# Squaring a second copy of the input: the head of a fused attention-and-experts block on one core

## Chip, cores and metric

The kernel runs on one core of a Trainium2 chip. The metric is the device time of one execution in microseconds (us), as the median of several executions. The profile shows one execution, taken by the hardware profiler.

## What is computed

One layer over 512 tokens of width 2048, all in float32. The part that matters here is its very beginning: the input is normalised and multiplied by a wide matrix, whose columns are then split into many projections.

```python
def rmsnorm(t, g):
    tf = t.astype(jnp.float32)
    y = tf * lax.rsqrt(jnp.mean(tf * tf, axis=-1, keepdims=True) + EPS)
    return (y * g.astype(jnp.float32)).astype(t.dtype)

def reference(x, positions, norm_mix_g, w_in, ...):
    ...
        h = rmsnorm(x, norm_mix_g[l])
        proj = jnp.einsum('bsd,de->bse', h, w_in[l])
        c_q, c_kv, k_rope, dq, dk, dv, iq, ik, iw, gates = jnp.split(proj, splits, axis=-1)
        o_a = mla_branch(c_q, c_kv, k_rope, ...)          # latent attention
        o_b = dsa_branch(dq, dk, dv, iq, ik, iw, ...)     # index scores, top-k, sparse attention
        gate = jax.nn.sigmoid(gates) ...
        merged = gate[:, :, 0, :] * (o_a @ w_branch_a[l]) + gate[:, :, 1, :] * (o_b @ w_branch_b[l])
        x = x + merged @ w_out[l]
        x = x + peer_ffn(rmsnorm(x, norm_ffn_g[l]), ...)  # 16384 experts, 128 picked per token
    return rmsnorm(x, norm_final_g)
```

## The kernel before

The tokens are worked in two halves of 256 (`HB`). `projections(i, ...)` does one half; `i = 0` is the first thing that the kernel does, and the change touches only that half, apart from a step that is written so that the second half keeps its place.

**Two-part products.** A float32 matrix product is made of three matmuls on rounded operands: a value is a high part (`hi`, a rounded copy, type fp32r) plus a low part (`lo`, what the rounding lost). `mm3` (L139 to L142) issues the three. `wload` (L106) loads a block of weights into `raw` (a ring of 4 buffers), lets ScalarE (ACT) make `hi` (ring of 4, L114) and VectorE (DVE) make `lo` (ring of 3, L115). `xraw` (L118) loads into the same `raw` ring without the split. Both are marked as high priority.

**Who sets the order.** The program is written as a stream of operations. A scheduler orders each engine's queue: among the operations that it takes to be ready it picks the one that comes first in the program, with the high-priority ones ahead. On the chip each engine then works its queue strictly in order. SyncE (SP) issues nearly all loads, in its own order.

**The first stage, for the first half.** Sixteen slices `k` of the transposed input (128 features x 256 tokens) come in four loads `in_xt` of 512 KB, and the weights of the first projection, `in_wdv`, in six loads. For each slice:

- ACT makes `hT` (L471), the high part of the slice times the gain `gmix`
- ACT makes `h1` (L473), an unsplit copy of the second 128 tokens of the same product, for the index queries further on
- DVE makes `lT` (L475), the low part
- ACT squares the slice (L478), and DVE adds the square to `sq` (L480)
- TensorE (PE) multiplies `hT` and `lT` with the weights into `pd` (L140 to L142 with 272 columns, 96 matmuls in all, two blocks of 128 tokens)

The gain is in `hT`, but 1/rms is not. It is found while PE goes on: one product with `ones` (`prr`, L505) sums `sq` over the partitions, `rstd_of` (L144 to L155) makes 1/rms of it on DVE and ACT, and the result lies in `rrow` (L507). Each later projection of this half is multiplied by `rrow` as it is read (`scaled`, L424).

After that stage the program has `angles(0)` and `angles(1)` (sines and cosines for the rotations; `angles(2)` stands inside the first stage, behind its first chunk, L481 to L487), then the projections. A projection chunk `proj_chunk` (L403) is 48 matmuls of 256 columns into `pm`, which has two buffers (tag `mm`; one of them is shared with `pd`). The first chunk is `W_KRIK` (result `xk`, followed by rotations L321 to L331), then the two gate chunks of feature block 0 (`gate`, L446), then eight index-query chunks with unsplit weights and `h1` (L546).

## Time and profile before

| | us |
|---|---|
| median of 3 runs | 3571.36 |
| the three runs | 3570.12, 3571.36, 3579.55 |
| the profiled execution, its time | 3575.54 |
| the profiled execution, its span | 3573.8 |

The span is from the first to the last instruction; 1.7 us lie around it. In the tables PE is TensorE's matmuls and PEld its weight loads, ACT ScalarE, DVE VectorE, SP SyncE (SPq its queue of DMA issues), PEclk the granted clock of TensorE as a share of full speed. L140 is line 140 of the kernel. A row of the timeline has start, duration, engine, line, operation, output and inputs, shape, count; in square brackets the idle time of the engine before it and what ended it. Durations are from start to end of an instruction, and neighbours on an engine overlap, so that the pitch (start to start) is shorter.

### The profile page before, as it was taken

The page shows a single profiled execution, that of the slowest core. Times are in us where ns is not written, and L with a number is a line of the kernel's source. Part 1 is how long each engine was busy: PE and PEld are TensorE (multiplying, and loading weights), DVE is VectorE, ACT ScalarE, POOL GpSimd, SP SyncE. Part 2 cuts the span into 40 slices and gives each one's busy share as a digit, 9 for nine tenths or more (in the row PEclk, how much of TensorE's full clock was granted, in tenths as well). Part 3 has the DMA queues.
Part 4 walks back from the last instruction along what each step waited for, and adds up shares of the span by engine and source line. Part 5 has one row for each costly group of instructions (what it writes and reads, how often), then busy time and mean ns, then how long its engine had stood idle before and what let it go on. Part 6 is the DMA issues. An engine that isn't in the chain of part 4 may idle for free.

```text
span 3573.8 us, 55133 instructions
## 1 busy us (share of the span) xinstructions
PE 3389.8 (95%) x20917; PEld 3041.6 (85%) x20917; DVE 2804.6 (78%) x4658; ACT 1428.7 (40%) x2195; POOL 581.8 (16%) x388
## 2 busy tenths in 40 slices
PE   8999899999889789899999999998999999999996
PEld 7999798778788679779999999998878778788885
DVE  6864565589997569878998887876878789788797
ACT  5454644443121453343354544543323233233232
POOL 0000000000222022210001111110322224223222
PEclk9999999999999989999999999999999999999998
DMA  6576267544999458976788888888989899999997
GB/s 221 187 227 207 73 208 243 168 148 174 346 369 393 171 193 339 355 293 223 250 308 313 330 328 325 325 320 332 367 321 346 328 365 349 354 357 352 355 357 284
DMA packets 282681, 1027.77 MB, mean 288 GB/s; under 512 B 29488, under 2 KB 98736, under 8 KB 228656
## 3 DMA queue, kind: packets, MB, share of 16 engines
q1 hardware_dynamic: 193712, 567.04, 45.1%
q0 software_dynamic: 55296, 402.68, 29.3%
q10 hardware_dynamic: 33408, 54.54, 4.1%
q8 instruction: 164, 2.69, 0.3%
q14 instruction: 101, 0.83, 0.1%
HBM read 962.80 MB, written 58.72 MB: 286 GB/s over the span
## 4 chain that ended last, share of the span: by engine, by line
PE 74%; DVE 11%; DMA 10%; ACT 2%; issue 2%; SPq 0%; ACTq 0%; DVEq 0%
PE pv L141 8%; PE pv L142 8%; PE pv L140 8%; PE pu L142 5%; PE pu L140 5%; PE pu L141 5%; PE pm L140 5%; PE pm L142 5%; PE pm L141 5%; PE pm L409 3%; DVE r L269 3%; DVE lo L115 3%; DMA gt<-g_d 3%; PE pg L939 2%; DMA raw<-in_win 2%
## 5 line engine op out<-in xcount | busy, mean ns | idle before, releaser
L114 ACT CAST hi<-raw 128x1024 fp32r<-128x1024 f32 (+2 forms) x836 | 873.4, 1049 | 1363.9 <-PE pv L142 298.5
L115 DVE TENSOR_TENSOR lo<-raw,hi 128x1024 fp32r<-128x1024 f32 (+2 forms) x836 | 1015.4, 1218 | 459.2 <-issue 128.2
L267 POOL DMA_INDIRECT r<-in_u,idx x256 | 367.7, 1436 | 2480.0 <-DVE dots L269 1397.5
L141 PE MATMUL pv<-lo,ch 128*128 128x512 f32 x1536 | 599.6, 392 | 18.9 <-DVE lo L115 18.8
L142 PE MATMUL pv<-hi,cl 128*128 128x512 f32 x1536 | 592.3, 391 | 0.0
L269 DVE CUSTOM_DVE_ANT_0 r<-r,h2g 128x2048 f32<-128x2048 f32 x256 | 582.3, 2284 | 10.0 <-DMA r<-in_u,idx 8.1
L140 PE MATMUL pu<-h2h,hi 128*128 128x256 f32 x1888 | 542.5, 287 | 10.8 <-ACT hi L114 8.3
L140 PE MATMUL pv<-hi,ch 128*128 128x512 f32 x1536 | 543.5, 391 | 2.3 <-ACT hi L114 1.6
L142 PE MATMUL pu<-h2h,lo 128*128 128x256 f32 x1888 | 533.9, 283 | 0.8 <-DVE lo L115 0.8
L141 PE MATMUL pu<-h2l,hi 128*128 128x256 f32 x1888 | 534.2, 283 | 0.0
L140 PE MATMUL pm<-hT,hi 128*128 128x256 f32 x1240 | 365.7, 295 | 18.0 <-ACT xi L421 7.7
L142 PE MATMUL pm<-hT,lo 128*128 128x256 f32 x1240 | 358.4, 289 | 14.2 <-DVE lo L115 14.2
L140 PEld LDWEIGHTS pu<-h2h,hi 128*128 128x128 f32 x1888 | 358.5, 190 | 12.0 <-ACT hi L114 8.5
L141 PEld LDWEIGHTS pv<-lo,ch 128*128 128x128 f32 x1536 | 290.2, 189 | 86.3 <-DVE lo L115 26.0
L142 PEld LDWEIGHTS pu<-h2h,lo 128*128 128x128 f32 x1888 | 358.3, 190 | 1.2 <-DVE lo L115 1.1
L141 PEld LDWEIGHTS pu<-h2l,hi 128*128 128x128 f32 x1888 | 358.5, 190 | 0.6
L141 PE MATMUL pm<-lT,hi 128*128 128x256 f32 x1240 | 355.0, 286 | 0.0
L140 PEld LDWEIGHTS pv<-hi,ch 128*128 128x128 f32 x1536 | 288.9, 188 | 64.2 <-ACT hi L114 2.9
L142 PEld LDWEIGHTS pv<-hi,cl 128*128 128x128 f32 x1536 | 290.1, 189 | 59.9
L282 DVE SCALAR_TENSOR_TENSOR hacc<-r,dots,hacc 128x2048 f32<-128x2048 f32 x128 | 300.4, 2347 | 9.7 <-DMA r<-in_v,idx 9.6
L280 POOL DMA_INDIRECT r<-in_v,idx x128 | 214.0, 1672 | 486.3 <-DVE hacc L282 393.0
L140 PEld LDWEIGHTS pm<-hT,hi 128*128 128x128 f32 x1240 | 239.2, 193 | 22.8 <-ACT xi L421 8.5
(396 smaller groups left out, 5278.6 us busy)
## 6 DMA issues: line engine op xcount, KB each, us to landing
raw<-in_ut SPq DMA_DIRECT2D x256, 512.0 KB
raw<-in_vd SPq DMA_DIRECT2D x256, 512.0 KB
raw<-in_win SPq DMA_DIRECT2D x228, 512.0 KB
raw<-in_wbr SPq DMA_DIRECT2D x64, 512.0 KB
raw<-in_wo SPq DMA_DIRECT2D x64, 512.0 KB
g_d<-gs ACTq DMA_DIRECT2D x24, 1024.0 KB
gt<-g_d SPq DMA_DIRECT2D x8, 3072.0 KB
raw<-in_wq SPq DMA_DIRECT2D x32, 512.0 KB
```

The costliest lines, as they stand in the source:

```text
L114: nc.scalar.copy(hi, raw)
L115: latest[0] = nc.vector.tensor_sub(lo, raw, hi.bitcast(F32))
L140: nc.tensor.matmul(ps, wh, xh, start=first, stop=False)
L141: nc.tensor.matmul(ps, wh, xl, start=False, stop=False)
L142: nc.tensor.matmul(ps, wl, xh, start=False, stop=last)
L267: nc.gpsimd.indirect_dma_start(out=r, out_offset=None, in_=a["u"], in_offset=bass.IndirectOffsetOnAxis(ap=idx[b][:, j:j + 1], axis=0))
L269: nc.vector.tensor_tensor_reduce(out=r, in0=r, in1=h2g[b], scale=1.0, scalar=0.0, op0=ALU.mult, op1=ALU.add, accum_out=dots[b][:, j:j + 1])
L280: nc.gpsimd.indirect_dma_start(out=r, out_offset=None, in_=a["v"], in_offset=bass.IndirectOffsetOnAxis(ap=idx[0][:, j:j + 1], axis=0))
L282: nc.vector.scalar_tensor_tensor(acc, r, dots[0][:, j:j + 1], acc, ALU.mult, ALU.add)
L409: nc.tensor.matmul(pm, w[:, j * P:(j + 1) * P], hF[:, j, :], start=False, stop=j == 7)
L939: end[0] = nc.tensor.matmul(pg[:, j], o2[:, j, :], og[:, j, :], start=True, stop=True)
```

## The change

It has five parts, all for the first half.

1. The squares (L478) and their additions (L480) leave the loop over the slices. Behind the first products the four blocks `in_xt` are loaded a second time, squared and added up.
2. The first two projection chunks (`W_KRIK` and the first gate chunk) are put ahead of that in the program, and so ahead of the product with `ones`.
3. The copy of `pd` into `dvw` (L518) is put ahead of these two chunks, as the second needs the buffer that `pd` holds.
4. The unsplit copy `h1` is no longer made by ACT from the input, but by DVE as `hT + lT`, behind the two gate chunks.
5. `angles(2)` with its loads (`fr`, `ident`, positions) stands behind the chunk of slices 12 to 14, no longer behind that of slices 0 to 2.

```diff
-                def gate(f, br):
+                def gate(f, br, pm=None):
...
-                    scaled(sg, proj_chunk(W_G + 2 * f + br), AF.Sigmoid)
+                    scaled(sg, pm or proj_chunk(W_G + 2 * f + br), AF.Sigmoid)
...
                             nc.scalar.activation(hT[:, k, :], x_, AF.Copy, scale=gmix[:, k:k + 1])
-                            if i == 0:
-                                nc.scalar.activation(h1[:, k, :], x_[:, P:], AF.Copy, scale=gmix[:, k:k + 1])
-                            if k < ks:
-                                nc.vector.scalar_tensor_tensor(lT[:, k, :], x_, gmix[:, k:k + 1], hT[:, k, :].bitcast(F32),
-                                                               ALU.mult, ALU.subtract)
-                            s2 = sq if k == 0 else dq[:, 4 + k % 4, :]
-                            nc.scalar.activation(s2, x_, AF.Square)
-                            if k:
-                                nc.vector.tensor_add(sq, sq, s2)
-                        if k0 == K_A:
+                            nc.vector.scalar_tensor_tensor(lT[:, k, :], x_, gmix[:, k:k + 1], hT[:, k, :].bitcast(F32),
+                                                           ALU.mult, ALU.subtract)
+                        if k0 == (0 if i else 12):
...
                     if i == 0:
+                        for j, tb in enumerate(blocks):
+                            nc.scalar.copy(dvw[:, tb, :], pd[j])
+                        first = [proj_chunk(m) for m in (W_KRIK, W_G)]
+                        for k in range(KT):
+                            if k % 4 == 0:
+                                xt = xraw(a["xt"][0, k // 4])
+                            s2 = sq if k == 0 else dq[:, 4 + k % 4, :]
+                            nc.scalar.activation(s2, xt[:, (k % 4) * HB:(k % 4 + 1) * HB], AF.Square)
+                            if k:
+                                nc.vector.tensor_add(sq, sq, s2)
                         pr = ps.tile([P, S], F32, name="prr", tag="tr")[:, :HB]
                         nc.tensor.matmul(pr, ones, sq, start=True, stop=True)
...
-                        nc.scalar.copy(dvw[:, tb, :], pd[j])
...
-                scaled(xk, proj_chunk(W_KRIK))
+                scaled(xk, proj_chunk(W_KRIK) if i else first[0])
...
                 for f in range(GF):
-                    gate(f, 0)
+                    gate(f, 0, None if i else first[1])
                     gate(f, 1)
+                if i == 0:
+                    for k in range(KT):
+                        nc.vector.tensor_add(h1[:, k, :], hT[:, k, P:].bitcast(F32), lT[:, k, P:].bitcast(F32))
```

## Rows read from the trace of the kernel before

**Rows 1.** The page: the span, and busy time of the engines with their share of the span.

```profile
span 3573.8 us, 55133 instructions
PE 3389.8 (95%) x20917; PEld 3041.6 (85%) x20917; DVE 2804.6 (78%) x4658; ACT 1428.7 (40%) x2195; POOL 581.8 (16%) x388
```

**Rows 2.** Busy time by stretch of the span: the stretch, its length, then busy us and count of PE, PEld, DVE, ACT and POOL, the granted clock, the share of the DMA engines and GB/s.

```profile
0.00:20.00 20.00, 9.91 (x54) 9.46 (x54) 14.28 (x36) 16.04 (x40) 0.20 (x4) 1.00 0.74 250
20.00:40.00 20.00, 17.54 (x130) 16.22 (x131) 17.24 (x29) 17.57 (x32) 0.00 (x0) 1.00 0.68 224
...
60.00:80.00 20.00, 19.96 (x148) 17.56 (x146) 9.85 (x36) 5.07 (x16) 0.00 (x0) 1.00 0.75 241
```

**Rows 3.** Timeline of PE: the first matmul, the first after the change of pitch, the waits of the first stage, the last product of `pd` and the first of `pm`, the product for 1/rms, the last of the second chunk, and the first rotation.

```profile
9.09 0.59 PE L140 MATMUL pd<-hi,hT 128*128 128x272 f32 x1 [9.09 <-ACT hT L471]
...
14.69 0.40 PE L140 MATMUL pd<-hi,hT 128*128 128x272 f32 x1
...
18.65 0.29 PE L142 MATMUL pd<-hi,lT 128*128 128x272 f32 x1
18.77 0.29 PE L140 MATMUL pd<-hi,hT 128*128 128x272 f32 x1
18.90 0.29 PE L141 MATMUL pd<-lo,hT 128*128 128x272 f32 x1
...
27.81 0.52 PE L140 MATMUL pd<-hi,hT 128*128 128x272 f32 x2 [1.15 <-ACT hi L114]
28.18 0.70 PE L505 MATMUL prr<-dq,ones 128*128 128x256 f32 x2
...
29.22 0.28 PE L140 MATMUL pm<-hT,hi 128*128 128x256 f32 x1
...
30.23 0.29 PE L140 MATMUL pm<-hT,hi 128*128 128x256 f32 x1
...
41.16 0.28 PE L142 MATMUL pm<-hT,lo 128*128 128x256 f32 x1
42.63 0.70 PE L321 MATMUL prot<-xk,cm 128*128 128x256 f32 x2 [1.19 <-DVE xk L424]
```

**Rows 4.** Groups of instructions by line and form, from 0 to 43 us: count, then busy us and mean ns of one, then idle time before them and what ended it.

```profile
L471 ACT ACTIVATE hT<-raw,gmix 128x256 fp32r<-128x256 f32 x16 | 7.9, 494 | 0.0
L475 DVE SCALAR_TENSOR_TENSOR lT<-raw,gmix,hT 128x256 fp32r<-128x256 f32 x16 | 7.5, 481 | 0.2 <-ACT hT L471 0.2
L480 DVE TENSOR_TENSOR dq<-dq 128x256 f32<-128x256 f32 x15 | 6.3, 422 | 0.5
L473 ACT ACTIVATE h<-raw,gmix 128x128 f32<-128x128 f32 x16 | 6.2, 386 | 0.0
L478 ACT ACTIVATE dq<-raw 128x256 f32<-128x256 f32 x16 | 6.0, 403 | 1.0 <-DMA raw<-in_xt 1.0
```

**Rows 5.** Timeline of ACT: the first split of weights, the second input block's first square and the first `hT`, and one later chunk of slices.

```profile
4.24 0.87 ACT L114 CAST hi<-raw 128x816 fp32r<-128x816 f32 x1 [2.22 <-DMA raw<-in_wdv]
...
8.22 0.42 ACT L478 ACTIVATE dq<-raw 128x256 f32<-128x256 f32 x1 [0.63 <-DMA raw<-in_xt]
8.54 0.49 ACT L471 ACTIVATE hT<-raw,gmix 128x256 fp32r<-128x256 f32 x1
...
24.05 0.49 ACT L471 ACTIVATE hT<-raw,gmix 128x256 fp32r<-128x256 f32 x1
24.45 0.39 ACT L473 ACTIVATE h<-raw,gmix 128x128 f32<-128x128 f32 x1
24.74 0.40 ACT L478 ACTIVATE dq<-raw 128x256 f32<-128x256 f32 x1
25.05 0.49 ACT L471 ACTIVATE hT<-raw,gmix 128x256 fp32r<-128x256 f32 x1
```

**Rows 6.** Timeline of DVE from the product for 1/rms to the first projection that it scales, with the first and the last of the five passes of `lo` between.

```profile
29.88 0.42 DVE L148 TENSOR_SCALAR rv<-prr 128x256 f32<-128x256 f32 x1
30.21 1.22 DVE L115 TENSOR_TENSOR lo<-raw,hi 128x1024 fp32r<-128x1024 f32 x1
31.34 0.35 DVE L434 TENSOR_SCALAR dq<-dq,fr 128x256 f32<-128x256 f32 x1
...
33.79 1.75 DVE L150 RECIPROCAL ry<-ry 128x256 f32<-128x256 f32 x1 [0.30 <-ACT ry L149]
...
39.08 1.22 DVE L115 TENSOR_TENSOR lo<-raw,hi 128x1024 fp32r<-128x1024 f32 x1
...
42.16 0.42 DVE L424 TENSOR_TENSOR xk<-pm,rrow 128x256 f32<-128x256 f32 x1
```

**Rows 7.** Timeline of SP: issues of the first input and weight blocks.

```profile
0.75 0.39 SPq L111 DMA_DIRECT2D raw<-in_wdv  x1
...
2.12 0.43 SPq L121 DMA_DIRECT2D raw<-in_xt  x1
2.60 0.53 SPq L401 DMA_DIRECT2D gmix<-in_gmix  x1
```

**Rows 8.** DMA from 0 to 120 us: GB/s in 40 slices of 3 us, and the total.

```profile
GB/s 91 384 372 368 154 125 188 223 179 158 274 343 236 240 158 0 44 113 273 287 288 203 225 268 229 204 295 173 264 301 349 261 190 180 156 172 68 220 116 202
DMA packets 9552, 25.73 MB, mean 214 GB/s; under 512 B 1552, under 2 KB 3344, under 8 KB 9542
```

**Rows 9.** A later place where PE waits (timeline of PE), and three stretches there with the columns of rows 2.

```profile
415.67 0.71 PE L640 MATMUL po<-pT,va 128*128 128x128 f32 x4 [0.39 <-ACT pT L638]
419.80 0.47 PE L355 MATMUL psc<-kr,two 128*128 128x128 f32 x1 [3.42 <-DMA two<-qrl]
...
420.00:424.00 4.00, 4.00 (x13) 3.08 (x13) 1.60 (x11) 1.80 (x7) 0.00 (x0) 0.50 0.00 0
...
428.00:432.00 4.00, 4.00 (x23) 4.00 (x24) 1.84 (x12) 3.33 (x12) 0.00 (x0) 0.58 0.00 0
430.00:434.00 4.00, 4.00 (x33) 4.00 (x31) 2.00 (x12) 3.81 (x15) 0.00 (x0) 0.83 0.00 0
```

**Rows 10.** Two neighbouring DVE operations on 128 x 128 elements in the index-query stage.

```profile
54.55 0.28 DVE L339 TENSOR_TENSOR rt<-xi,trig 128x128 f32<-128x128 f32 x1
54.75 0.28 DVE L340 TENSOR_TENSOR rt<-rt,trig 128x128 f32<-128x128 f32 x1
```

## The prediction

> **What bounds the kernel now.** I read the page first: PE is busy 95% of the span [rows 1], so over the whole kernel a change counts only where PE waits or runs slowly. The diff touches only the first 50 us or so, so I read that stretch next, by the table of stretches. From 60 us on PE is busy all the time (19.96 of 20 us), from 0 to 20 it is busy 9.91 and from 20 to 40 it is busy 17.54, with ACT at 16.04 and 17.57 and DVE at 14.28 and 17.24 [rows 2]. So what happens before PE becomes the bound moves the end by the same amount, and nothing later gives it back.
>
> The timeline of PE says how much there is to win [rows 3]. PE's first matmul is at 9.09; the first rotation, which needs `xk` and so 1/rms, is at 42.63, and from there PE is full again. I take 42.63 as the mark: what the change does to it is what it does to the time. Between lie 33.54 us. The work in them, at the fast pitch: 96 matmuls of `pd` at 0.125 (18.65, 18.77, 18.90) are 12.0; 96 of the two chunks at 0.1175 (from 30.23 to 41.16 are 93 steps) are 11.3; the two of `prr` are 0.7. That is 24.0. The first 24 matmuls ran at a pitch of 0.23, from 9.09 to 14.69, 5.6 us where the fast pitch needs 3.0: 2.6 more. So 33.54 - 24.0 - 2.6 = 6.9 us are waits and gaps, 1.2 of them the last wait, for `xk`. **No version of this stage that starts at 9.09 can win more than 6.9 us, 0.19% of the time.** What a measurement of this kernel can tell from no change is about 0.3%, or 10.7 us.
>
> **Part by part.** *ACT in the first stage.* For each slice ACT makes `hT`, `h1` and the square, at pitches of 0.40, 0.29 and 0.31: 24.05 to 25.05, 1.00 us for a slice [rows 5]. The change leaves 0.40. Sixteen slices lose 9.6 us of ACT, and DVE loses 15 additions [rows 4] at a pitch of about 0.34, 5.1 us. For a chunk of three slices ACT then needs about 0.77 + 1.2 = 2.0 us against 18 x 0.125 = 2.25 of PE. So ACT, which most of PE's waits in this stage named, falls behind PE as the bound. The start stays: the first `hT` at 8.54 stands behind a square that waited for the second input block, but the load of `gmix`, which `hT` needs, was issued behind that block [rows 5, 7]; at most 0.3 us are to be had, and I take none. With the slow clock until 14.69 and 72 matmuls left, `pd` ends at 14.69 + 9.0 = 23.7 at the earliest, where the last ended at 29.2. Gain 5.5 at most; I take 4.5 for waits that stay, since loads and the split on DVE have the same rate as PE now. The bounds are 3.5 and 5.5.
>
> *The two chunks* need 11.3 us whether they run before or behind `prr`. They end at 35.0 at the earliest, 37.0 at the latest; I take 36.0.
>
> *The product for 1/rms.* Before, it ran at 28.18, among the last matmuls of `pd`, and everything that follows from it lay under the two chunks [rows 3, 6]. Now it stands behind them in the program. Their matmuls are ready all the time, and an engine's queue takes the earlier in the program first, so I place it behind the second chunk: 36.0 to 36.7. The squares are there by then: `raw` has four buffers, and a weight block leaves its buffer when `lo` is made, which needs one of three `lo` buffers, so the fourth weight block goes when PE is through the first half chunk, 2.8 us behind 24.7, at 27.5. The last input block is issued then. The nearest load with nothing ahead of it took from 0.75 to 4.24, 3.5 us [rows 5, 7]; 31.0, and four squares and an addition are 1.6 more: 32.6. These 2 MB hide under the chunks with 3 us to spare.
>
> *The chain behind it.* From 29.88 to the end of `xk` at 42.58 are 12.7 us, but five passes of `lo` on DVE lie between its links, of about 1.14 pitch each, 5.7 us [rows 6]. In the changed order no weight block waits to be split at that point, as the next blocks with a split are few and early and the index queries have none. So 7.0 is the upper bound. The links alone are `rv` 0.42, the square root 0.42, 1.75 for the reciprocal, four more short operations of 1.3 together, the copy 0.28 and `xk` 0.42, in sum about 4.6, with steps between engines 4.8: the lower bound. I take 6.2, nearer to the upper, as sines and cosines still fill DVE's holes. Now nothing covers it: PE has no other buffer for `pm`, and the third chunk waits for `xk`. So `prr` begins at 36.0, 0.7 + 6.2 + 0.1 later the rotation: 43.0, or **0.4 later than before**. By the bounds it is 35.0 + 5.6 = 40.6 (2.0 earlier) to 37.0 + 7.8 = 44.8 (2.2 later).
>
> *The clock in that wait.* PE stands idle 5 to 7 us. The nearest row is a wait of 3.42 us up to 419.80, behind which the granted clock is 0.50, that is 1.2 GHz, until some 431, then 2.4 GHz [rows 9]. So I expect half speed behind the new wait. What it costs is bounded by two rows: the start, 2.6 us more over 5.6 us of full work [rows 3], and that later place, where some 11.7 us at half clock would cost 5.9 for full work [rows 9]. The third chunk is full work as at the start, so I take 2.5.
>
> The Trainium skill, "TensorE: Matmul & The Clock Gate", section "What's actually happening", says that the throttled state is the default and that activity releases it; so a wait does more harm than its length. The trace agrees at 419.80 (0.50 after 3.42 us of idling). By that rule the sum is 2.9 us later; if the clock stayed at full the rotation's 0.4 would be all.
>
> *`h1` on DVE.* Sixteen additions of 128 x 128 at a pitch of 0.20 [rows 10] are 3.2 us; they must be done when the index queries start, about 8 us behind the rotation. They need only `hT` and `lT`, so DVE's holes during the chunks and the chain can take them. I take zero; uncovered they cost up to 3.2.
>
> *The other edits* move `angles(2)` and the copy of `pd`. The sines are wanted only at the rotation, and the copy (two ACT operations) comes before the second chunk needs its buffer, 6 us later: nothing, and at most the 1.3 us by which a table load for the sine could hold a split.
>
> **Sum.** -4.5 for `pd`, + 11.3 + 0.7 and a chain that is no longer under the chunks: together +0.4 at the rotation; +2.5 for the clock; 0 for `h1`: **+2.9 us**. Against the profiled execution's 3575.5 that is 3578.4, against the median of the runs, which is 4.2 lower, 3574.3. I forecast 3575 us, no change that can be measured. Its own range is -2.0 to +8.1 on these two bases, some 3569 to 3583.
>
> **Rivals.**
>
> *The early result.* 1/rms is found under the second chunk, because `prr` is put between its matmuls as soon as the squares are there, 32.6. The chain needs to 39.4 to 40, so the wait is only about 3 us, and the clock holds: the rotation comes 3 to 5.5 us earlier, 3566 to 3571 us. For it speaks that before `prr` was slipped among matmuls of `pd` [rows 3]; against it that those matmuls were waiting for a split at that moment (1.15 us at 27.81) and these are not.
>
> *The late squares (slower).* The second reading is 2 MB more on the same queue and in the same four buffers. Up to the last square 4.2 MB of first-stage loads, 0.8 of constants, 2.1 of weights and 2.1 of second reading must come, 9.2 MB. At the 370 to 380 GB/s of 3 to 12 us this takes 25 us and hides; at the mean of the first 120 us, 214 GB/s [rows 8], it takes 43 and the rotation comes at about 51, 8 later, plus 2.5 to 5.9 of clock: +11 to +14, 3582 to 3590. It decides from a last square at about 42 us. Against it: before, that low mean comes from buffers that waited for PE or ACT, not from the engines of the DMA.
>
> *DVE takes it over.* From 8.5 to 50 us the additions, splits, `lT`, squares, `angles` and the chain add up to about as much as there is time. If `h1` comes last, the first index query waits up to 3.2 us on top of the forecast: +3 to +6, 3574 to 3582.
>
> *The change does not shorten the first stage* at all, as the loads pace it and not ACT: `pd` ends at 28 or later, and the uncovered chain puts the rotation at 47, +4.5 and clock: 3579 to 3584.
>
> **How the numbers follow.** Forecast 0.62, early result 0.15, DVE 0.10, late squares 0.06, no shortening 0.07. The three runs shown lie within 9.4 us of one another, as much as all of these but the late squares are worth. The range takes the forecast's own, the early result (3566 less some scatter) and no shortening: 3564 to 3584. Faster by over 0.3% is beyond the 6.9 us of the stage and would need something later in the kernel to fall better as well, 0.06; slower by over 0.3% is the late squares and part of no shortening, 0.09; the rest, 0.85, is no change.
>
> **What would show it.** The last matmul of `pd` at 24 to 25.5; `prr` behind the last matmul of the second `pm`, at 35 to 37; PE's wait for `xk` at 5 to 7 us instead of 1.19; matmuls of the third chunk at a pitch of 0.23; the index queries' first matmul 0 to 5 us later than 50.2. It is wrong if `prr` stands among the second chunk's matmuls, if a wait of `prr` names the input's second load, if the first stage still ends behind 27, or if the head is unchanged and a later stage moved.

## The result, and the profile after the change

The changed kernel took 3596.13 us (median of 5 runs, 3589.56 to 3599.23) against 3572.34 for the kernel before (5 runs, 3570.12 to 3579.55): a ratio of 1.006, 95% interval 1.0045 to 1.0075. It is slower, by 22 us on the mean and 23.8 on the median; forecast were 3575 us and a range up to 3584. The page after, its span and its busy times [rows 1 before]:

```profile
span 3593.5 us, 55125 instructions
PE 3395.0 (94%) x20917; PEld 3042.2 (85%) x20917; DVE 2806.3 (78%) x4674; ACT 1424.3 (40%) x2178; POOL 591.8 (16%) x388
```

The same matmuls were made, and no engine is much busier, so the time went into waits of PE. The timeline of PE after shows all that are above 0.25 us up to the first rotation, and the last product of `pd` (last in brackets: idle time before the instruction, and what ended it):

```profile
9.08 0.59 PE L140 MATMUL pd<-hi,hT 128*128 128x272 f32 x1 [9.08 <-ACT hT L471]
...
23.78 0.39 PE L140 MATMUL pm<-hT,hi 128*128 128x256 f32 x1 [0.41 <-ACT hi L114]
...
24.50 0.29 PE L142 MATMUL pd<-hi,lT 128*128 128x272 f32 x1
25.04 0.39 PE L142 MATMUL pm<-hT,lo 128*128 128x256 f32 x1 [0.26 <-DVE lo L115]
...
43.12 1.22 PE L508 MATMUL prr<-dq,ones 128*128 128x256 f32 x2 [6.34 <-DVE dq L506]
...
51.60 1.22 PE L321 MATMUL prot<-xk,cm 128*128 128x256 f32 x2 [7.26 <-DVE xk L424]
```

In the kernel before, the last product of `pd` stands here (timeline of PE before):

```profile
29.09 0.29 PE L142 MATMUL pd<-hi,lT 128*128 128x272 f32 x1
```

Against it and [rows 3]: the first matmul stands where it stood, the last product of `pd` comes 4.6 us earlier, and the first product of `pm` at 23.78 and not at 29.22, 5.4 us earlier. PE has done both chunks at about 36.8, and then waits twice: 6.34 us until the last addition of squares is made, and 7.26 us for `xk`. The first rotation begins at 51.60, 9.0 later than at 42.63. The two products behind each wait are recorded with 1.22 us where [rows 3] have 0.70, which is half speed. The table of stretches (columns of [rows 2]) says the same:

```profile
0.00:50.00 50.00, 28.19 (x194) 26.62 (x194) 38.61 (x95) 31.35 (x57) 0.20 (x4) 0.92 0.75 251
50.00:100.00 50.00, 48.07 (x356) 44.38 (x357) 25.38 (x88) 14.50 (x36) 0.00 (x0) 0.94 0.58 183
...
43.00:55.00 12.00, 4.62 (x14) 3.54 (x15) 9.84 (x32) 5.46 (x10) 0.00 (x0) 0.50 0.16 56
```

The granted clock is 0.92 and 0.94, and between 43 and 55 us it is 0.50, that is 1.2 GHz. Matmul by matmul against the profile of before, PE is 11.1 us late on the median from 50 to 100 us, that is 2.1 more than at the rotation, and 12.5 between 200 and 350 ("Does it repeat?" below says what the last step is). At the end it is 22 late in this execution.

Why the sum is late is seen in DVE's timeline:

```profile
30.66 1.48 DVE L506 TENSOR_TENSOR dq<-dq 128x256 f32<-128x256 f32 x3
33.23 0.30 DVE L443 TENSOR_SCALAR dq<-dq 128x256 f32<-128x256 f32 x1 [1.09 <-ACT dq L442]
33.44 0.95 DVE L506 TENSOR_TENSOR dq<-dq 128x256 f32<-128x256 f32 x2
...
38.15 1.23 DVE L115 TENSOR_TENSOR lo<-raw,hi 128x1024 fp32r<-128x1024 f32 x1
39.30 0.42 DVE L439 SCALAR_TENSOR_TENSOR dq<-dq 128x256 f32<-128x256 f32 x1
39.63 0.42 DVE L506 TENSOR_TENSOR dq<-dq 128x256 f32<-128x256 f32 x1
39.97 1.22 DVE L115 TENSOR_TENSOR lo<-raw,hi 128x1024 fp32r<-128x1024 f32 x1
...
42.65 0.42 DVE L506 TENSOR_TENSOR dq<-dq 128x256 f32<-128x256 f32 x1
...
44.37 0.42 DVE L148 TENSOR_SCALAR rv<-prr 128x256 f32<-128x256 f32 x1 [0.42 <-PE prr L508]
46.16 1.75 DVE L150 RECIPROCAL ry<-ry 128x256 f32<-128x256 f32 x1 [0.78 <-ACT ry L149]
51.13 0.42 DVE L424 TENSOR_TENSOR xk<-pm,rrow 128x256 f32<-128x256 f32 x1
```

The fifteen additions (L506) run from 30.66 to 43.07. Among them lie both splits of the third chunk (L115, 1.2 each) and steps of `angles` (L434 to L443). ACT's last square is made at 40.00. At no square does its timeline name a load of the second reading as what ended a wait. It does show two costs of the `angles`: a table load among the squares (for the sines of `angles(2)`, which part 5 of the change has moved here) and one in the chain to 1/rms:

```profile
29.51 1.34 ACT L504 ACTIVATE dq<-raw 128x256 f32<-128x256 f32 x4
30.87 1.28 ACT L441 ACT_TABLE_LOAD   x1
...
35.24 1.43 ACT L504 ACTIVATE dq<-raw 128x256 f32<-128x256 f32 x3 [0.20 <-DVE dq L506]
37.08 1.04 ACT L114 CAST hi<-raw 128x1024 fp32r<-128x1024 f32 x1 [0.40 <-DMA raw<-in_win]
...
39.59 0.41 ACT L504 ACTIVATE dq<-raw 128x256 f32<-128x256 f32 x1
...
44.42 1.28 ACT L149 ACT_TABLE_LOAD   x1
45.72 0.42 ACT L149 ACTIVATE ry<-rv 128x256 f32<-128x256 f32 x1
```

SP issued the four blocks of the second reading from 25.02 to 30.88 (29.44 the third, 30.88 the fourth).

### The profile page after: what moved, and what is told of

Its sections match the earlier page's. It is cut to its first block, busy times and chain, and to the rows that moved or that the text cites. A ratio compares the mean times of both kernels' runs of the same rounds, so it can differ in the third digit from the quotient of the medians.

```text
span 3593.5 us, 55125 instructions
## 1 busy us (share of the span) xinstructions
PE 3395.0 (94%) x20917; PEld 3042.2 (85%) x20917; DVE 2806.3 (78%) x4674; ACT 1424.3 (40%) x2178; POOL 591.8 (16%) x388
## 4 chain that ended last, share of the span: by engine, by line
PE 69%; DVE 14%; DMA 9%; issue 5%; ACT 2%; POOL 0%; SPq 0%; ACTq 0%; DVEq 0%; POOLq 0%
PE pv L141 8%; PE pv L142 8%; PE pv L140 8%; PE pu L142 5%; PE pu L141 5%; PE pu L140 5%; PE pm L140 4%; PE pm L142 4%; PE pm L141 4%; DVE lo L115 3%; DVE r L269 3%; DMA raw<-in_win 2%; DMA gt<-g_d 2%; PE pg L944 2%; PE pm L409 2%
## 5 line engine op out<-in xcount | busy, mean ns | idle before, releaser
L115 DVE TENSOR_TENSOR lo<-raw,hi 128x1024 fp32r<-128x1024 f32 (+2 forms) x836 | 1015.2, 1219 | 463.0 <-issue 129.5
L140 PE MATMUL pm<-hT,hi 128*128 128x256 f32 x1240 | 367.1, 296 | 16.8 <-ACT xi L421 5.8
L142 PE MATMUL pm<-hT,lo 128*128 128x256 f32 x1240 | 360.1, 291 | 13.6 <-DVE lo L115 13.5
L280 POOL DMA_INDIRECT r<-in_v,idx x128 | 226.0, 1766 | 480.6 <-DVE hacc L282 396.1
```

What stands on the lines that cost most here:

```text
L115: latest[0] = nc.vector.tensor_sub(lo, raw, hi.bitcast(F32))
L140: nc.tensor.matmul(ps, wh, xh, start=first, stop=False)
L142: nc.tensor.matmul(ps, wl, xh, start=False, stop=last)
L280: nc.gpsimd.indirect_dma_start(out=r, out_offset=None, in_=a["v"], in_offset=bass.IndirectOffsetOnAxis(ap=idx[0][:, j:j + 1], axis=0))
```

## Experiments

"Mean difference" is the mean of a kernel's runs less that of the runs of the kernel before in the same job, with its standard error. "Head" is the median lateness of PE's matmuls between 200 and 350 us of the span against the profile of before, that is what the head of the kernel has cost; two profiles of one program differ in it by 1 to 2. All in us; the whole is in a table at the end of this section.

**Does it repeat?** e1 and e15 are the changed kernel unaltered.

> The changed kernel once more, unaltered. In its trace the first rotation stands at 51.6 us (42.6 before) and the stages behind some 300 us are about 12 us later than before; by the end of the span it is 20 to 22 later. Theory A: the loss behind the head comes from the order of the queues, which differs from before all along the kernel and is the same in every execution of this program; then this profile shows the same steps again, +3 near 2945 us, +4 near 3175, +2 near 3350, and the median is again 20 to 25 us above before. Theory B: the later steps are chance of one execution; then they stand at other places and the runs scatter by as much.

> The changed kernel, unaltered, a third time. If what it loses behind the head (some 7 us by the medians) belongs to its order, the median is 18 to 22 us above before again, with 12.5 at 250 us. If it is chance of the earlier runs, the median falls to 11 to 14.

e1: 3591.26 us, ratio 1.0051 (1.0033 to 1.0069); e15: 3589.49, 1.0045 (1.003 to 1.0059). The head repeats (rotation at 51.86 and 53.46; cost 13.4 and 12.6). At the end of the profile PE was 12.1 and 14.0 late, not 22. In the first profile 10 us more had gathered in steps near 2945, 3175 and 3350 us; those belonged to that one execution. That the other two end less late than the runs' mean has to do with which executions were profiled: e1's is the fastest of its six runs (3585.0, their mean 3590.2), and that of before is of a run 3 us above the mean of its kind (3575.5; the mean in e1's job is 3572.7). Over the 19 runs of the three jobs the change costs 18.4 ± 1.1 us.

Some 1 us of the head is not the change's. Against the one profile of before, PE falls behind by 1.2 to 1.3 us between 120 and 240 us in the first profile of the changed kernel and in e1, but also in e14, which is the kernel before unaltered; in e15 it does not. Without that drift the head of the three profiles costs 11.2, 12.1 and 12.6. The heads of e3 to e6, e8, e9 and e16 hold it too.

**Is a late head carried to the end?** In e2 and e5 the kernel before only starts late: `gmix`, which the first `hT` needs, is loaded in many pieces of 4 bytes, 2,048 of them in e2, as shown, and 26,624 in e5, where 208 values are loaded for each partition in place of 16.

```diff
-                    nc.sync.dma_start(gmix, a["gmix"])
+                    nc.sync.dma_start(gmix, a["gmixw"].rearrange("p (k w) -> p k w", w=16)[:, :, 0])
```

> The kernel before with one edit: the gain vector comes by 2048 small pieces, so that the first high part, and all behind it, starts some us later. The queues of PE, ACT, DVE and POOL hold the same instructions in the same order as before. If the loss of the change is made in the head and only carried on, a late start of d us costs d us at the end, within 3 us. Theory A (order) says so: whatever the start loses is the whole loss, nothing is added behind. Theory B (a shift makes later stages collide with their transfers): the end is later by d plus 8 to 12 us.

> The kernel before with the gain vector in 26624 small pieces (the first 16 columns are used). At the rate of the smaller version, some 2500 pieces per us, the first high part waits for about 10 us more. Behind the first some 150 instructions of PE's queue the order is that of the kernel before. PE's first matmul then comes at 17 to 20 us, the first rotation d = 7 to 11 us later than in the kernel before. Theory A (what the changed kernel loses beyond its head comes from its other order): the end is later by d within 3 us. Theory B (a shift of some 10 us alone makes later stages collide): the end is later by d plus 6 to 10.

e2 came only 0.4 late (3574.08, 1.0004, 0.9991 to 1.0017): too little to decide anything. In e5 ACT stood still for it, and the first matmul was at 24.13:

```profile
23.57 0.51 ACT L471 ACTIVATE hT<-raw,gmix 128x256 fp32r<-128x256 f32 x1 [14.25 <-DMA gmix<-in_gmixw]
```

The rotation was 16.5 late (7 to 11 were expected), the head 20.3, the time 22.8 ± 4.1 (1.0065, 1.0041 to 1.0089). Of the 3.8 us between rotation and head, 2.4 come with a granted clock below full up to 70 us, and 1.3 are the drift. A late head is carried to the end at about its own size, within the error of 4; that step of the forecast holds.

**What makes the sum late?** e3 is the changed kernel with only the first of the four blocks read again and squared; twelve squares and their additions are left out.

```diff
-                        for k in range(KT):
+                        for k in range(4):
```

> The changed kernel, but only the first of the four input blocks is read a second time, squared and added (12 squares, 12 additions and three loads are left out, so the mean that it forms is of four slices). My theory: PE's wait of 6.3 us for the sum is the loads, squares and additions of the last three blocks behind sines and splits; without them the product for 1/rms follows the second chunk at once, at 36 us, and the first rotation comes at 43 to 44.5, 7 to 8.5 earlier than in the changed kernel; with a slow clock behind the wait that stays. Rival: the wait is one for the second chunk's buffers or for ACT's table; then the rotation stays at 49 or later.

No wait for the sum is left, and the wait for `xk` is as long as before (timeline of PE):

```profile
38.81 0.59 PE L508 MATMUL prr<-dq,ones 128*128 128x256 f32 x2
46.65 1.22 PE L321 MATMUL prot<-xk,cm 128*128 128x256 f32 x2 [7.24 <-DVE xk L424]
```

The rotation came at 46.65, later than I expected, as the second chunk itself waited 1.36 for its weights. Against the changed kernel the three further blocks are worth 5.0 us at the rotation and some 10 in the time (18.4 ± 1.1 less the 8.1 ± 1.6 that is left).

In e4 the sines of `angles(0)` and `angles(1)` stand behind `xk` on DVE.

```diff
-                angles(0)
-                angles(1)
...
-                scaled(xk, proj_chunk(W_KRIK) if i else first[0])
+                    with tc.issue_after(nc.vector.tensor_mul(xk, first[0], rrow).ins):
+                        angles(0)
+                        angles(1)
```

> The changed kernel with the sines and cosines of angles(0) and angles(1) put behind xk in DVE's queue. Nothing is left out. Behind the head its queues stand as in the changed kernel. My theory: DVE makes the additions late because ten operations of angles(0) (3.4 us at their pitch) stand between them, and the chain is long because those of angles(1) and two table loads of 1.28 stand in it; so the product for 1/rms comes at 39 to 40 us in place of 43.1, the rotation at 45 to 46.5 in place of 51.6, and the end 5 to 6 us earlier than the changed kernel. Rival: the additions are late because the last block lands late; then the product stays at 42 to 43 and the rotation at 49 to 50.

The chain became shorter, the sum hardly earlier (timeline of PE, and below it what a query of the second reading's line says of its loads):

```profile
42.30 1.22 PE L508 MATMUL prr<-dq,ones 128*128 128x256 f32 x2 [4.78 <-DVE dq L506]
48.84 1.22 PE L321 MATMUL prot<-xk,cm 128*128 128x256 f32 x2 [5.32 <-DVE xk L532]
```

```profile
L121 SPq DMA_DIRECT2D raw<-in_xt x4: 327/328/328, 24.9 to 31.6; - x4
...
DMA to landing us min/median/max: 3.2/4.6/5.3
```

The sines cost the chain 1.9 us (7.26 to 5.32). Of the late sum they are a small part: `prr` is 0.8 earlier, not three. It helps to count from the first square to the end of the last addition, since the first square itself comes at 29.51, 29.93 and 31.52 in the three profiles of the changed kernel, behind the splits of the second chunk's weights. So counted the changed kernel takes 13.6, 13.4 and 13.4 us, and e4, from 30.25, takes 12.0. The four loads take 3.2 to 5.3 us and not 3.5, 4.6 on the median. The last is issued at 31.6; it landed at 35.5, 4.5 behind the forecast's 31.0 and still 6.8 ahead of `prr`.

e6 puts the second reading, the product and the chain ahead of both chunks in the program.

```diff
-                        first = [proj_chunk(m) for m in (W_KRIK, W_G)]
                         for k in range(KT):
...
+                        first = [proj_chunk(m) for m in (W_KRIK, W_G)]
```

> The changed kernel with the second reading, the squares, the product for 1/rms and its chain put ahead of the two projection chunks in the program. PE's queue then has the product behind the first chunk in place of behind the second. My theory: what costs is that the chain for 1/rms stands behind both chunks; with the second chunk behind the product, PE waits for the sum before it, until some 34 to 36 us, and the chain runs under the second chunk; the first rotation comes at 42 to 44, as before the change, with no slow clock, and the end is within 4 us of the kernel before plus what the other order adds. Rival: the second reading itself is late whatever the order; then PE waits for it to 40 or later and the rotation stays at 47 or later.

```profile
31.75 0.58 PE L140 MATMUL pm<-hT,hi 128*128 128x256 f32 x1 [7.83 <-ACT hi L114]
...
39.21 0.59 PE L507 MATMUL prr<-dq,ones 128*128 128x256 f32 x2
50.35 1.22 PE L321 MATMUL prot<-xk,cm 128*128 128x256 f32 x2 [4.38 <-DVE xk L424]
```

PE loses 7.83 at another place: the weights of the first chunk now stand behind the second reading in the queue of loads and in the ring of four buffers. The rotation is at 50.35, where I expected 42 to 44; 3586.09 us, 1.0037 (1.0025 to 1.005). In this order PE waits for no sum, but for weights that are issued from 24.57 on and not from 18.46.

e9 is e4 with the third chunk's two splits behind the last square and the last addition as well.

```diff
+                    if i == 0:
+                        with tc.issue_after(last_sq.ins), tc.issue_after(last_add.ins):
+                            third = proj_chunk(W_G + 1)
...
```

> The kernel of the run with the sines behind xk, and in addition the splits of the third chunk's two weight blocks are put behind the last square on ACT and behind the last addition on DVE. There, ACT made a split of 1.03 at 37.60 before the last two squares, and DVE made two of 1.22, at 38.75 and 40.23, before the last additions; the product for 1/rms came at 42.30. My theory: of the wait for the sum 3 to 4 us are these splits; the product comes at 38.5 to 39.5, right behind the second chunk, and the first rotation at 44.5 to 46 (48.84 there). Rival: the last block lands late enough, 35.5 there, that the sum is late anyway; then the product comes at 41 or later and the rotation at 47.5 or later.

```profile
34.63 6.24 DVE L506 TENSOR_TENSOR dq<-dq 128x256 f32<-128x256 f32 x12
40.78 2.35 DVE L115 TENSOR_TENSOR lo<-raw,hi 128x1024 fp32r<-128x1024 f32 x2
43.05 0.42 DVE L148 TENSOR_SCALAR rv<-prr 128x256 f32<-128x256 f32 x1
```

Nothing stands between the last twelve additions now (timeline of DVE), and the sum takes 10.2 us from the first square (30.70), 1.8 less than in e4. Still `prr` came at 40.92, behind a wait of 4.06, where I expected 38.5 to 39.5. The additions go at a pitch of 0.52, each on the result of the one ahead. The squares can't run far ahead, since they have four buffers that the additions free. So the dependent additions may themselves be a cause. And the splits now stand in front of `rv`, where they cost 0.9 (from `prr` to the rotation 7.41 us, in e4 6.54).

e13 tests that: e9 with four separate sums, each square added to the sum of its place, and two additions that join them. From the fifth on a square is written over its own input, so that the four buffers no longer bind either.

```diff
-                                last_add = nc.vector.tensor_add(sq, sq, s2)
+                            x_, s4 = xt[:, (k % 4) * HB:(k % 4 + 1) * HB], dq[:, 4 + k % 4, :]
+                            last_sq = nc.scalar.activation(s4 if k < 4 else x_, x_, AF.Square)
+                            if k >= 4:
+                                nc.vector.tensor_add(s4, s4, x_)
+                        nc.vector.tensor_add(dq[:, 4:6, :], dq[:, 4:6, :], dq[:, 6:8, :])
+                        last_add = nc.vector.tensor_add(sq, dq[:, 4, :], dq[:, 5, :])
```

> The kernel of the run with the splits behind, with the squares added into four separate sums that are joined at the end by two additions. There the 15 additions into one sum stood at a pitch of 0.52 back to back (12 in 6.24 us), each waiting for the one before, and the squares, with four buffers, waited for them; the product for 1/rms came at 40.92. My theory: this chain sets the end of the sum; at a pitch of 0.34 the additions keep up with ACT and the product comes at 38 to 39, the first rotation at 45 to 46.3 (48.33 there). Rival: the last block lands at 35.5 or later and its squares set the end; the product stays at 40 or later.

Timeline of DVE, then of PE, then of ACT:

```profile
36.37 2.95 DVE L506 TENSOR_TENSOR dq<-dq,raw 128x256 f32<-128x256 f32 x8
39.36 0.69 DVE L507 TENSOR_TENSOR dq<-dq 128x512 f32<-128x512 f32 x1
40.08 0.43 DVE L508 TENSOR_TENSOR dq<-dq 128x256 f32<-128x256 f32 x1
40.42 2.52 DVE L115 TENSOR_TENSOR lo<-raw,hi 128x1024 fp32r<-128x1024 f32 x2
42.86 0.42 DVE L148 TENSOR_SCALAR rv<-prr 128x256 f32<-128x256 f32 x1
```

```profile
30.11 0.39 PE L140 MATMUL pm<-hT,hi 128*128 128x256 f32 x1 [2.04 <-ACT hi L114]
...
40.56 0.70 PE L510 MATMUL prr<-dq,ones 128*128 128x256 f32 x2 [0.32 <-DVE dq L508]
48.13 1.22 PE L321 MATMUL prot<-xk,cm 128*128 128x256 f32 x2 [6.87 <-DVE xk L534]
```

```profile
31.41 1.34 ACT L504 ACTIVATE dq<-raw 128x256 f32<-128x256 f32 x4
32.77 1.28 ACT L441 ACT_TABLE_LOAD   x1
34.06 0.42 ACT L441 ACTIVATE trig<-dq 128x256 f32<-128x256 f32 x1
...
37.46 1.32 ACT L504 ACTIVATE raw<-raw 128x256 f32<-128x256 f32 x4
```

The pitch is 0.37, and from the first square (31.41) the sum takes 9.1 us, 1.1 less than in e9: that is what the dependence and the four buffers are worth together. The wait for the sum is 0.32 in place of 4.06, but not for that reason. The sum was ready at 40.51, only 0.4 earlier than in e9 (40.87); it was the second chunk that ended later, at 40.24 in place of 36.86, because it had waited 2.04 for its weights, which landed late. `prr` came at 40.56, where I expected 38 to 39, and so within what the rival said (40 or later). The landing that the rival named does not hold the sum, though: the last block landed at 36.52, and its squares began at 37.46. What sets the end now is ACT, whose timeline shows no pause from the first square to the end of the last at 38.78, with a table load and three steps of `angles(2)` among them, 2.2 us. No run takes those out. The rotation is won by 0.2 only, as the two splits still stand in front of `rv`. e13 loses 10.8 ± 2.3, which can't be told from the 11.7 ± 1.6 of e9.

**One part alone.** e7 and e16 are one kernel: the changed one without the second reading, with the squares in the first loop as before.

```diff
+                            s2 = sq if k == 0 else dq[:, 4 + k % 4, :]
+                            nc.scalar.activation(s2, x_, AF.Square)
+                            if k:
+                                nc.vector.tensor_add(sq, sq, s2)
                         if k0 == (0 if i else 12):
...
```

> The changed kernel without its second reading: the squares and additions stand in the first loop again, the unsplit copies stay on DVE behind the gates, and the two chunks stay ahead of the product for 1/rms. My theory: the first products end at 26 to 27 (ACT makes two operations for each slice), the sum is there by then, but the product stands behind the second chunk in PE's queue, so that it comes at 37 to 38.5 and the chain is uncovered: rotation at 44.5 to 46.5, 2 to 4 later than before, plus some 2 for the slow clock. Rival (the second reading is the whole loss): the rotation comes at 42.6 or earlier.

> The kernel that reads once, with both chunks ahead of the product, a second time. Its head lost 3.9 us and its median 16.8. If the rest belongs to its order, the median is 12 to 18 above before again; if it is chance, 3 to 7.

```profile
38.22 0.59 PE L505 MATMUL prr<-dq,ones 128*128 128x256 f32 x2
45.09 1.22 PE L321 MATMUL prot<-xk,cm 128*128 128x256 f32 x2 [6.27 <-DVE xk L424]
```

The head does what was expected: no wait for the sum, the uncovered chain of 6.27, the rotation 2.5 late and the head 3.9 and 6.1. The time does not: 15.0 ± 2.3 and 18.6 ± 2.2 slower, twice 11 to 13 more than the head.

e8 is the kernel before with `h1` made by GpSimd (POOL) as `hT + lT` in the first loop.

```diff
-                                nc.scalar.activation(h1[:, k, :], x_[:, P:], AF.Copy, scale=gmix[:, k:k + 1])
+                                nc.gpsimd.tensor_add(h1[:, k, :], hT[:, k, P:].bitcast(F32), lT[:, k, P:].bitcast(F32))
```

> The kernel before with one edit: the unsplit copies are made by GpSimd as the sum of high and low part, in the first loop. Nothing is read again and nothing else is moved. ACT loses 16 operations of 0.29 pitch, 4.6 us, so the first products end 1.5 to 3 us earlier. PE's queue has the product for 1/rms three quarters through the two chunks, some 9 us behind the first products. My theory: a gain in the first products is spent again, since the chain now starts at 34 to 35 and takes 7: rotation at 41 to 43, the end within 2 us of the kernel before plus what the other order adds. Rival: the gain stays, rotation at 40 or earlier.

It was a little slower, not faster: 3576.27, 1.0015 (1.0005 to 1.0025), rotation at 44.87, where I expected 41 to 43. `prr` went late into the second chunk (36.97), so the chain was uncovered here too (a wait of 4.34). Nor did the first products end much earlier: the last of `pd` is at 28.42 in place of 29.09.

**Does the order behind the head cost something by itself?** Where the head changes, the scheduler places instructions of DVE, ACT and SP otherwise all along the kernel. To see what another order alone does, e10, e11 and e12 add 8, 16 and 30 matmuls ahead of the last index query (`h` = 15) of the first half, which nothing needs. With 8, the order behind stays that of before; with 16 and 30 it differs. e14 is the kernel before unaltered.

```diff
+                            for _ in range(8 if i == 0 and h == 15 else 0):
+                                nc.tensor.matmul(pi, two[hh][:, qs], ik[0][:, :n], start=True, stop=True)
```

> The kernel before with eight matmuls of 256 columns more, of about 0.3 us each, at the end of the index queries of the first half, where PE sets the time. All queues behind them stand as in the kernel before. Both theories: PE is about 2.5 us later there. Theory A (the order of the queues makes what is lost or won behind the head): with the same order the end is later by 2 to 4 us, no more. Theory B (any shift changes how later stages meet their transfers): the end can be off by 8 us either way.

> As the run with eight matmuls more, with sixteen, about 5 us. With these the scheduler makes another order of all queues from there on. Theory A: the end differs from 5 us later by an amount of its own that belongs to this order, between 6 less and 10 more, and its runs agree on it within their scatter. Theory B or no effect of order: 5 us later within 3.

> As the run with sixteen matmuls more, with thirty, about 9.5 us, again with an order of its own. Theory A: the end is later by 9.5 us and an amount of its own, between 6 less and 10 more, other than that of sixteen. No effect of order: 9.5 us later within 3.

> The kernel before, unaltered, for a second profile. Both executions hold the same work in the same order; the head agrees within 0.5 us. If later steps are a property of the program, they agree within 2 us along the kernel; if executions scatter, offsets of up to 5 us come and go behind 350 us, and the runs spread over 15 to 20 us as before.

The excess of the mean difference over the head is -0.2 in e10, and 2.7 and 2.8 in e11 and e12, with errors of 1.3 to 1.8. The added matmuls themselves cost about half of what I had put: the head is 1.3, 2.9 and 4.6 late where I expected 2.5, 5 and 9.5. Two profiles of the kernel before differ by -4.6 to +1.9 along the way (medians of 100 us).

| run | rotation | head | mean difference | order behind the head |
|---|---|---|---|---|
| changed, e1, e15 | 51.6, 51.9, 53.5 | 12.5, 13.4, 12.6 | 22.0 ± 2.3, 17.5 ± 1.8, 16.8 ± 1.8 | its own |
| e2 | 43.0 | 0.3 | 1.9 ± 2.0 | of before |
| e5 | 59.2 | 20.3 | 22.8 ± 4.1 | of before |
| e10 | 43.2 | 1.3 | 1.1 ± 1.6 | of before |
| e14 | 42.3 | 1.0 | -0.8 ± 1.7 (ratio 0.9999, 0.9985 to 1.0012) | of before |
| e3 | 46.7 | 7.8 | 8.1 ± 1.6 | nearly that of e6 |
| e4 | 48.8 | 10.4 | 14.8 ± 1.5 | nearly that of the changed |
| e6 | 50.4 | 11.6 | 13.1 ± 1.8 | another |
| e7, e16 | 45.1, 45.3 | 3.9, 6.1 | 15.0 ± 2.3, 18.6 ± 2.2 | another |
| e8 | 44.9 | 6.0 | 4.2 ± 1.4 | nearly that of e6 |
| e9 | 48.3 | 13.8 | 11.7 ± 1.6 | another |
| e13 | 48.1 | 8.6 | 10.8 ± 2.3 | another |
| e11, e12 | 42.7, 42.9 | 2.9, 4.6 | 5.6 ± 1.8, 7.4 ± 1.3 | another |

With the order of before, head and time agree within 2.5 us. With another they differ by -2.1 to +4.4, except in the changed kernel (9.5, then 4.1 and 4.2; 5.6 ± 1.1 over its 19 runs) and in e7 and e16 (11.1 and 12.5). The traces also show which kernels share an order: of all runs of six neighbouring DVE instructions behind 62 us, e3, e6 and e8 have 98% or more in common, e4 and the changed kernel 99%, and no other two of these orders more than 95%. The excess goes with that: 0.3, 1.5 and -1.8 in e3, e6 and e8, whose heads differ by 5.6; 4.4 in e4 beside the 5.6 of the changed kernel. (Where a head holds the drift, its excess is some 1.2 larger without it.)

## Why the prediction was wrong

*The first stage* was right: `pd` was done 4.6 us earlier, within the 3.5 to 5.5, and the chunks ended at 36.8, within 35 to 37 (at 37.2 and 38.8 in e1 and e15, where their weights landed later). The rival without a shorter stage is out.

*The place of the product* was right in kind: it stands behind the second chunk, and the early result did not happen, not even in e6.

***The sum over the squares* is the step that failed.** "These 2 MB hide under the chunks with 3 us to spare": ready at 32.6, said the forecast; it was ready at 43.07, 10.5 later, and `prr` 7.1 later than 36.0. The term that was mis-sized is the work between the loads and the sum: I put four squares and one addition, 1.6 us, behind the last landing, as if ACT and DVE kept up with the loads. The last block was late as well (issued at 30.88, not 27.5; in e1 at 31.29, and landed at 35.82, not 31.0), but ACT's timelines show no square that waited for it. From the first square to the end of the last addition the two engines took 13.4 to 13.6 us in three profiles, where sixteen squares at their pitch of 0.31 [rows 5] and one addition are 5.4. Three experiments show what the rest is made of: without the sines of `angles(0)` and `angles(1)` it was 12.0 (e4), without the splits too 10.2 (e9), without the dependence and the four buffers as well 9.1 (e13). What is left in e13 is ACT's squares with the table load and the three steps of `angles(2)` among them, 7.4 us, and 1.7 for the last additions. So two more sentences of the forecast were false: "in the changed order no weight block waits to be split at that point" (the third chunk's two did), and that moving `angles(2)` costs nothing. None of the three kernels had the sum ready before 40.5, since the first square came later in each (30.25, 30.70, 31.41).

*The late squares* were the rival with the right place and nearly the right price (+11 to +14; the head cost 12.5). Its last square "at about 42 us" was made at 40.0 to 41.9. But its mechanism was another: it asked for a slow DMA. The window's 251 GB/s lies nearer to its 214 than to 370, yet from the landing, at 35.82 in e1, to the sum at 43.33 there are 7.5 us that are ACT's and DVE's. I gave it 0.06, because I weighed it against the DMA alone. The rival that had DVE as the bound priced only `h1`, which did hide (all sixteen additions lie between 10.1 and 25.2); the additions were the load that mattered.

*The chain* took 7.26 of wait where 6.2 were forecast and 7.0 was the bound: 1.28 of it is a table load for the square root, behind the cosine of `angles(0)`. The trace of before has that load too (at 32.04 on ACT), and the sum of the links left it out. Counted from `prr` to the rotation it is 8.5 against 7.0, of which 0.5 is `prr` at half clock.

*The clock* was sized well: 2.1 behind the rotation against 2.5 (2.9 and 1.5 in e1 and e15). The granted clock was 0.50 from 43 to 55 us, behind the two waits. The Trainium skill, "TensorE: Matmul & The Clock Gate", section "What's actually happening", has it that idling brings the throttle back; the trace agrees, with 1.22 for two products that took 0.70 before.

So the head: 7.1 for the late sum and 1.5 for the chain on top of the forecast's 0.4 give 9.0 at the rotation, with the clock 11.1. The 12.5 from 200 us on hold 1.3 of the drift that the kernel before shows as well.

*"Nothing later gives it back"* held (e5), but something was added. The measured 18.4 us are 5.6 ± 1.1 more than the head. The forecast took the kernel behind the head as fixed, and its range had no term for queues that are ordered anew. That this excess can be 11 to 13 us is shown for e7 and e16, one kernel measured twice; that the order is its cause is concluded and not shown: a late head alone does not make it (e5), kernels with nearly one order have nearly one excess, but no run changes an order alone by so much (e11 and e12 do it for 2.7 ± 1.8 and 2.8 ± 1.3). Where in the kernel it arises stays open: behind 350 us the profiles of one program scatter by several us, as much as what is looked for.

## What to carry to other kernels

Work that is put "under" a busy engine must be costed on the engine that does it, in that engine's queue order, to its last instruction: here no square was seen to wait for the second reading's loads, and the squares and additions were late all the same, among sines, splits and additions that each needed the one ahead. A result that everything waits for belongs where another stage covers its whole chain; once the product for 1/rms stood behind the chunks, each of its links was on the path, and so was whatever else those engines had been given to do. And in a kernel whose order a scheduler writes, a change at the head deals the later queues anew: allow some us on both sides for that (the excess went from -2 to +12 here), and measure a kernel with the same head and the old order before the whole difference is put down to the edit.

## What the runs showed of the hardware

- Additions of 128 x 256 on DVE, each needing the one ahead, go at a pitch of 0.52 us (12 in 6.24); independent ones at 0.37 (8 in 2.95). An instruction is recorded as 0.42 in both cases, so its duration does not tell. Separate sums, and with them free buffers for the squares, were worth 1.1 us of a sum of 10.2 (e9 to e13).
- A load of 26,624 pieces of 4 bytes kept its user idle for 14.25 us (e5), one of 2,048 made the first rotation 0.4 later (e2).
- Behind waits of 6.3 and 7.3 us TensorE went on at half clock (0.50 granted from 43 to 55 us); that cost 2.1, 2.9 and 1.5 us behind the rotation in three profiles.
- One program's PE can fall behind by some 1 us between 120 and 240 us in one execution and not in another, at a granted clock of 1.00 in both (before and e14). The cause is open.
